# Two transformer blocks on one core: the second feed-forward in interleaved blocks of three, its later value chunks transposed by VectorE

## The chip, the core and the metric

One program runs on one core of a Trainium2 chip. The metric is the device time of one execution in microseconds (us), lower is better. TensorE multiplies, VectorE (DVE) and ScalarE (ACT) work element by element, GpSimd (POOL) has little to do here, and SyncE (SP) issues the transfers of the weights. Each engine takes its instructions in the order in which the program lists them, and waits on semaphores for the others.

## The reference, cut to what matters

Two blocks follow each other on 256 tokens of width 2048, in float32. The second block ends with a feed-forward part, and the change lies wholly in it:

```python
def conv_ffn(h, w_up, conv_w, conv_b, w_down):      # h: 256 x 2048
    u = h @ w_up                                    # w_up: 2048 x 11264
    ...
    y = conv_b                                      # causal, width 3, each channel by itself
    for i in range(CONV_WIDTH_2):
        y = y + conv_w[i] * u_pad[:, i:i + S]
    gate, val = jnp.split(y, 2, axis=-1)            # 5632 channels each
    return (jax.nn.silu(gate) * val) @ w_down       # w_down: 5632 x 2048
```

Its result is added to `x`, and that is the output.

## The kernel before

**Chunks, tiles, units, steps.** Every matrix product is cut into chunks of 512 output columns (`CW`), which accumulate in one of two PSUM buffers (`acc`). A chunk's contraction is cut into tiles of 512 rows of weights, and each tile into two units of 256 rows. A unit has two steps of 128 rows. An up chunk (512 columns of `w_up`) has 4 tiles, so 8 units and 16 steps; the 22 up chunks come in pairs, a gate chunk `g` and a value chunk `v` with the same index j from 0 to 10. A pair makes 512 of the 5632 rows that the down product contracts over (`d0` to `d10`). A down chunk is 512 columns of `w_down` over the rows of one block of pairs, with one tile for each pair of the block.

**Precision.** All products are made of float32r parts: the weights are split into `wh` (rounded, a copy by ScalarE, line 846) and `wl` (what is left, a subtraction by VectorE, line 847), the left-hand side in the same way into the two halves of a tile `k_...`. Of each step, TensorE issues six products of 512 columns (line 887): four with `wh`, then two with `wl`. The split of a unit is put into the program three units before its products (`SPLIT_AHEAD = 3`); `wh`, `wl` and the raw weights have four buffers each.

**The order of the other work.** `later(delay, fn)` puts a piece of work on a heap, due so many steps from now; after each step at most three due pieces are put into the program (`run_due`). At the end of a chunk its `evac` is put in, ahead of what is due. `need` puts in everything up to a key at once. The place of an instruction in the engine's queue is fixed by this, long before the kernel runs.

**What an up chunk leaves to do** (`evac_up`): ScalarE copies the accumulator to `z` with the tokens on the partitions (line 440). Then `z` is transposed, since the convolution and the down product want the channels there. This is done in one of two ways:

- `transposed`: TensorE makes four 128 x 128 transposes at a time into a PSUM tile `p_t` (line 175), two such groups for a chunk, due 3 and 5 steps after its end (2 and 3 for the last value chunk, `soon`).
- `turned`: VectorE makes 16 transposes of 32 x 256 into an SBUF tile `z_t` (line 190), two after each step from the second on (`rate=2`).

The convolution follows for each half of the chunk: ScalarE's part (line 479), four operations of VectorE (line 484). For a gate chunk comes a sigmoid by ScalarE (line 745) and a product by VectorE (line 746). For a value chunk comes the product with the gate (VectorE, line 740) and the split into the `k_d` tile (ScalarE line 155, VectorE line 162). Before the change all gate chunks are `turned` and all value chunks `transposed`.

**A down chunk** leaves one addition by VectorE of 128 x 1024 elements to the residual `x` (`evac_add`, line 543). The last chunk of the program is computed half by half (`acc_last`, lines 893 to 895 and 540).

**The order of chunks** is that of the calls of `add_chunk`: four pairs, then four down chunks of 4 tiles; four pairs, four down chunks of 4 tiles; three pairs, four down chunks of 3 tiles.

Of the kernel before, what the change touches and what calls it, by code (L numbers as in the profile page):

```python
# [26 lines left out]
FF2 = 5632  # L27
EPS = 1e-6
NEG = -1e30
CW = 512  # L30
# [31 lines left out]
def tile_two_blocks(  # L62
# [30 lines left out]
    def later(delay, fn, *keys):  # L93
        seq[0] += 1
        heapq.heappush(tasks, (now[0] + delay, seq[0], fn, keys))

    def chain(delay, stages, *keys, gap=1):

        for i, fn in enumerate(stages):
            later(delay + i * gap, fn, *(keys if i == len(stages) - 1 else ()))  # L100
# [11 lines left out]
    def need(*keys):  # L112
        for key in keys:
            while key not in ready:
                run_one()
# [21 lines left out]
    def add_chunk(w, row0s, c0, ncol, acts, evac):  # L137

        chunks.append((w, row0s, c0, ncol, acts, evac))
# [7 lines left out]
    def split_out(key, j, n, p, scales=None):  # L147

        if key not in K:
            kt_tile(key)  # L150
        hi, lo = (K[key][:, h, j:j + n, :] for h in range(2))

        def to_hi():
            if scales is None:
                S.copy(hi, p)
            else:
                for i in range(n):
                    S.activation(hi[:, i, :], p[:, i, :], AF.Copy, scale=scales[i])

        def to_lo():  # L160
            if scales is None:
                V.tensor_tensor(out=lo, in0=p, in1=hi.bitcast(F32), op=OP.subtract)  # L162
            else:
                for i in range(n):
                    V.scalar_tensor_tensor(out=lo[:, i, :], in0=p[:, i, :], scalar=scales[i],  # L165
                                           in1=hi[:, i, :].bitcast(F32), op0=OP.mult, op1=OP.subtract)
        return [to_hi, to_lo]

    def transposed(z, use, delay, keys=(), gap=1, lag=1, step=1):

        def task(b, mine):
            p = tr_p.tile([P, 2, T], F32, tag="tr", name="p_t")
            for j in range(2):
                for tb in range(TB):
                    TE.transpose(p[:, j, tb * P:(tb + 1) * P], z[:, tb, (2 * b + j) * P:(2 * b + j + 1) * P], ident)  # L175
            chain(lag, use(b, p), *mine, gap=step)
        for b in range(2):
            later(delay + gap * b, lambda b=b: task(b, keys[2 * b:2 * b + 2]))

    def turned(z, use, delay, keys, rate=3, lag=1):  # L180

        t = {}

        def part(i0, i1):
            if i0 == 0:
                t["o"] = z_p.tile([P, 4, T], F32, tag="z", name="z_t")
            for q, j in [divmod(i, 4) for i in range(i0, i1)]:
                src = z[32 * q:32 * q + 32].rearrange("p b (k c) -> p b k c", c=P)[:, :, :, 32 * j:32 * j + 32]
                dst = t["o"][32 * j:32 * j + 32].rearrange("p k (b t) -> p b k t", b=TB)[:, :, :, 32 * q:32 * q + 32]
                V.transpose(dst, src)  # L190

        def rest():
            for b in range(2):
                chain(lag + b, use(b, t["o"][:, 2 * b:2 * b + 2, :]), *keys[2 * b:2 * b + 2])
        n = 0
        for i in range(0, 16, rate):
            later(delay + n, lambda i=i: part(i, min(i + rate, 16)))
            n += 1
        later(delay + n - 1, rest, keys[0] + " turned")

    def group_keys(key):
        return [f"{key} {j}" for j in range(4)]
# [174 lines left out]
    hT = lambda name: [f"{name}{n}" for n in range(4)]  # L377
# [57 lines left out]
    def evac_scaled(rname, then, mult=None):  # L435

        def evac(acc):
            z = z_p.tile([P, TB, CW], F32, tag="z", name="z")
            for tb in range(TB):
                S.activation(z[:, tb, :], acc[:, tb, :], AF.Copy, scale=R[rname][:, tb:tb + 1])  # L440
            then(z)
        return evac
# [32 lines left out]
    def conv3(o, u, w, bias):  # L475

        def last():
            for i in range(2):
                S.activation(o[:, i, :], u[:, i, :], AF.Identity, bias=bias(i), scale=w(i, 2))

        def before():
            for i in range(2):
                for d in (1, 2):
                    V.scalar_tensor_tensor(out=o[:, i, d:T], in0=u[:, i, 0:T - d], scalar=w(i, 2 - d), in1=o[:, i, d:T],  # L484
                                           op0=OP.mult, op1=OP.add)
        return [last, before]
# [50 lines left out]
    def evac_add(n, then=None):  # L537
        def evac(acc, tb=None):
            if tb is not None:
                V.tensor_tensor(out=xs[n][:, tb, :], in0=xs[n][:, tb, :], in1=acc, op=OP.add)  # L540
                nc.sync.dma_start(outr[:, tb, n * CW:(n + 1) * CW], xs[n][:, tb, :])
                return
            V.tensor_tensor(out=xs[n], in0=xs[n], in1=acc, op=OP.add)
            if then:
                then(n)
        return evac
# [182 lines left out]
    def evac_up(which, j, key):  # L729
        def then(z):  # L730
            cv = z_p.tile([P, 4, T], F32, tag="z", name="z_cv")

            def use(b, p):
                a = cv[:, 2 * b:2 * b + 2, :]
                c0 = (0 if which == "g" else 44) + 4 * j + 2 * b
                steps = conv3(a, p, lambda i, t: ccol[:, t, c0 + i:c0 + i + 1], lambda i: ccol[:, 3, c0 + i:c0 + i + 1])
                if which == "v":
                    g = FU["g", j][:, 2 * b:2 * b + 2, :]
                    need(f"gate{j} {2 * b}")
                    return steps + [lambda: V.tensor_tensor(out=a, in0=a, in1=g, op=OP.mult), *split_out(key, 2 * b, 2, a)]  # L740
                t = {}

                def sigmoid():
                    t["s"] = s_p.tile([P, 2, T], F32, tag="s", name="sg")
                    S.activation(t["s"], a, AF.Sigmoid)
                return steps + [sigmoid, lambda: V.tensor_tensor(out=a, in0=a, in1=t["s"], op=OP.mult)]
            if which == "g":
                FU["g", j] = cv
            if which == "g":
                turned(z, use, 2, group_keys(f"gate{j}"), rate=2)  # L750
            else:
                soon = j == FF2 // CW - 1
                transposed(z, use, 2 if soon else 3, group_keys(key), gap=1 if soon else 2)
        return then


# [2 lines left out]
    G4 = [0, 512, 1024, 1536]  # L759
# [27 lines left out]
    for blk in range(4):  # L787
        for i in range(4):
            j = 4 * blk + i
# [18 lines left out]
    def store(n):  # L808
        nc.sync.dma_start(outr[:, :, n * CW:(n + 1) * CW], xs[n])

    j = 0
    for cnt in (4, 4, 3):
        js = list(range(j, j + cnt))
        j += cnt
        for jj in js:
            add_chunk(w_up_2[0], G4, jj * CW, CW, hT("g"), evac_scaled("r4", evac_up("g", jj, f"d{jj}")))
            add_chunk(w_up_2[0], G4, FF2 + jj * CW, CW, hT("g"), evac_scaled("r4", evac_up("v", jj, f"d{jj}")))
        for n in range(4):
            add_chunk(w_down_2[0], [jj * CW for jj in js], n * CW, CW, [f"d{jj}" for jj in js],
                      evac_add(n, store if j == 11 else None))  # L820


    wtiles = []
# [137 lines left out]
```

## Time and profile before

| | us |
|---|---|
| median of 3 runs (2393.58 to 2395.01) | 2394.24 |
| the profiled execution's own time | 2393.52 |
| its span, first to last instruction | 2391.8 |
| TensorE busy in the span | 2362.4 |
| VectorE busy | 1662.8 |
| ScalarE busy | 1159.0 |

The second feed-forward runs from 1654 us of the span to its end. Times in the profile are counted from the start of the span; the 1.7 us between the span and the execution's own time lie outside it. A matmul's end is modelled, so the distance of two starts is a better measure of TensorE than its busy time.

### The profile page before, as it was taken

The page shows a single profiled execution, that of the slowest core. Times are in us where ns is not written, and L with a number is a line of the kernel's source. Part 1 is how long each engine was busy: PE and PEld are TensorE (multiplying, and loading weights), DVE is VectorE, ACT ScalarE, POOL GpSimd, SP SyncE. Part 2 cuts the span into 40 slices and gives each one's busy share as a digit, 9 for nine tenths or more (in the row PEclk, how much of TensorE's full clock was granted, in tenths as well). Part 3 has the DMA queues.
Part 4 walks back from the last instruction along what each step waited for, and adds up shares of the span by engine and source line. Part 5 has one row for each costly group of instructions (what it writes and reads, how often), then busy time and mean ns, then how long its engine had stood idle before and what let it go on. Part 6 is the DMA issues. An engine that isn't in the chain of part 4 may idle for free.

```text
span 2391.8 us, 27807 instructions
## 1 busy us (share of the span) xinstructions
PE 2362.4 (99%) x10649; PEld 1960.1 (82%) x10649; DVE 1662.8 (70%) x2293; ACT 1159.0 (48%) x1514; POOL 36.7 (2%) x53
## 2 busy tenths in 40 slices
PE   9899999999999999999999999999999999999999
PEld 9688888888888888888888888888888888888887
DVE  5487776665877567567578857668788568864884
ACT  5355454444455344344354455545555345554553
POOL 1000000000000000000000001000000000000000
PEclk9999999999999999999999999999999999999999
DMA  7755656655556556656555666555555656565553
GB/s 259 188 184 165 204 194 207 202 201 177 192 195 195 193 181 206 193 184 201 193 183 190 189 205 203 165 176 194 183 177 199 199 180 206 178 198 189 194 185 132
DMA packets 230966, 456.67 MB, mean 191 GB/s; under 512 B 8085, under 2 KB 15997, under 8 KB 230832
## 3 DMA queue, kind: packets, MB, share of 16 engines
q1 hardware_dynamic: 227584, 445.81, 56.7%
q0 software_dynamic: 3248, 9.08, 1.6%
q8 instruction: 83, 1.36, 0.2%
q14 instruction: 51, 0.42, 0.0%
HBM read 451.18 MB, written 3.67 MB: 190 GB/s over the span
## 4 chain that ended last, share of the span: by engine, by line
PE 91%; DVE 4%; DMA 2%; ACT 1%; issue 1%; SPq 0%; POOL 0%; ACTq 0%; DVEq 0%
PE acc L887 89%; DMA raw<-in_w_in_dram 2%; DVE wl L847 2%; DVE z_t L190 1%; ACT wh L846 1%; PE p_t L175 1%; PE acc_last L887 0%; DVE z_cv L484 0%; PE p_t L360 0%; PE p_s L316 0%; PE p_t L714 0%; DVE k_i L165 0%; PE p_p L351 0%; ACT junk L227 0%; DMA bg<-in_g_final_dram 0%
## 5 line engine op out<-in xcount | busy, mean ns | idle before, releaser
L847 DVE TENSOR_TENSOR wl<-raw,wh 128x1024 fp32r<-128x1024 f32 (+1 forms) x848 | 1021.6, 1214 | 635.1 <-ACT wh L846 546.5
L846 ACT CAST wh<-raw 128x1024 fp32r<-128x1024 f32 (+1 forms) x848 | 876.5, 1044 | 713.6 <-PE acc L887 648.9
L887 PE MATMUL acc<-wh,k_g 128*128 128x512 f32 x1408 | 378.4, 390 | 0.0
L887 PE MATMUL acc<-wh,k_h 128*128 128x512 f32 (+1 forms) x1344 | 352.2, 384 | 12.6 <-ACT wh L846 12.2
L887 PEld LDWEIGHTS acc<-wh,k_g 128*128 128x128 f32 x1408 | 263.0, 188 | 53.8
L887 PEld LDWEIGHTS acc<-wh,k_h 128*128 128x128 f32 x1344 | 247.2, 189 | 58.3 <-ACT wh L846 13.5
L887 PE MATMUL acc<-wh,k_u 128*128 128x512 f32 x1024 | 274.8, 390 | 4.5 <-DVE k_u L162 4.5
L887 PE MATMUL acc<-wh,k_f 128*128 128x512 f32 x1024 | 273.9, 389 | 0.0
L887 PEld LDWEIGHTS acc<-wh,k_u 128*128 128x128 f32 x1024 | 191.9, 188 | 45.9 <-DVE k_u L162 6.2
L887 PEld LDWEIGHTS acc<-wh,k_f 128*128 128x128 f32 x1024 | 192.1, 188 | 39.8
L887 PE MATMUL acc<-wl,k_g 128*128 128x512 f32 x704 | 216.9, 389 | 0.0
L887 PE MATMUL acc<-wl,k_h 128*128 128x512 f32 (+1 forms) x672 | 201.1, 380 | 0.1
L887 PE MATMUL acc<-wh,k_d 128*128 128x512 f32 x656 | 176.3, 390 | 1.5 <-DVE k_d L162 1.5
L887 PE MATMUL acc<-wl,k_u 128*128 128x512 f32 x512 | 157.7, 389 | 0.0
L887 PE MATMUL acc<-wl,k_f 128*128 128x512 f32 x512 | 157.6, 389 | 0.0
L887 PEld LDWEIGHTS acc<-wl,k_g 128*128 128x128 f32 x704 | 132.1, 188 | 27.8
L190 DVE STREAM_TRANSPOSE z_t<-z 32x256 f32<-32x256 f32 x336 | 146.3, 435 | 5.6
L887 PEld LDWEIGHTS acc<-wh,k_d 128*128 128x128 f32 x656 | 122.6, 188 | 27.1 <-DVE k_d L162 1.9
L887 PEld LDWEIGHTS acc<-wl,k_h 128*128 128x128 f32 x672 | 125.0, 188 | 23.6 <-DVE wl L847 0.7
L887 PE MATMUL acc<-wh,k_i 128*128 128x512 f32 x512 | 141.0, 398 | 0.6 <-ACT wh L846 0.6
L190 DVE STREAM_TRANSPOSE z_t<-z_f 32x256 f32<-32x256 f32 x256 | 111.4, 435 | 4.1
L887 PEld LDWEIGHTS acc<-wl,k_u 128*128 128x128 f32 x512 | 96.1, 188 | 20.0
(227 smaller groups left out, 2006.3 us busy)
## 6 DMA issues: line engine op xcount, KB each, us to landing
raw<-in_w_ff_dram SPq DMA_DIRECT2D x128, 1024.0 KB, 5.2
raw<-in_w_in_dram SPq DMA_DIRECT2D x104, 1024.0 KB, 5.1
raw<-in_w_up_dram SPq DMA_DIRECT2D x88, 1024.0 KB, 5.1
raw<-in_w_down_dram SPq DMA_DIRECT2D x44, 1024.0 KB, 5.2
raw<-in_w_mix_out_dram SPq DMA_DIRECT2D x16, 1024.0 KB, 5.1
raw<-in_w_out_dram SPq DMA_DIRECT2D x16, 1024.0 KB, 5.1
raw<-in_w_conv_out_dram SPq DMA_DIRECT2D x8, 1024.0 KB, 5.2
raw<-in_w_attn_out_dram SPq DMA_DIRECT2D x8, 1024.0 KB, 5.3
```

What stands on the lines that cost most here:

```text
L175: TE.transpose(p[:, j, tb * P:(tb + 1) * P], z[:, tb, (2 * b + j) * P:(2 * b + j + 1) * P], ident)
L190: V.transpose(dst, src)
L846: S.copy(wh[:, :, 0:ncol], raw)
L847: V.tensor_tensor(out=wl[:, :, 0:ncol], in0=raw, in1=wh[:, :, 0:ncol].bitcast(F32), op=OP.subtract)
L887: TE.matmul(halves[tb][:, 0:ncol], k[:, i, kt, tb * P:(tb + 1) * P], w[:, kk, 0:ncol], start=begin and first and kt == 0, stop=end and stop)
```

## The change

Two things are changed. The order of chunks: the pairs form blocks of three (0 to 2, 3 to 5, 6 to 8, and 9 and 10); after the first block, each following pair of up chunks is followed by one down chunk of the block before, and what is left of the four down chunks comes behind the block's last pair. The down chunks of the first three blocks have 3 tiles (12 steps), those of the last block 2 tiles (8 steps). And the value chunks from j = 3 on are `turned` (VectorE) instead of `transposed` (TensorE); the three before keep TensorE, and the special case for the last one is gone.

```diff
             if which == "g":
                 turned(z, use, 2, group_keys(f"gate{j}"), rate=2)
+            elif j >= 3:
+                turned(z, use, 2, group_keys(key), rate=2)
             else:
-                soon = j == FF2 // CW - 1
-                transposed(z, use, 2 if soon else 3, group_keys(key), gap=1 if soon else 2)
+                transposed(z, use, 3, group_keys(key), gap=2)
...
-    j = 0
-    for cnt in (4, 4, 3):
-        js = list(range(j, j + cnt))
-        j += cnt
-        for jj in js:
-            add_chunk(w_up_2[0], G4, jj * CW, CW, hT("g"), evac_scaled("r4", evac_up("g", jj, f"d{jj}")))
-            add_chunk(w_up_2[0], G4, FF2 + jj * CW, CW, hT("g"), evac_scaled("r4", evac_up("v", jj, f"d{jj}")))
+    def up_chunks(j):
+        add_chunk(w_up_2[0], G4, j * CW, CW, hT("g"), evac_scaled("r4", evac_up("g", j, f"d{j}")))
+        add_chunk(w_up_2[0], G4, FF2 + j * CW, CW, hT("g"), evac_scaled("r4", evac_up("v", j, f"d{j}")))
+
+    def down_chunk(js, n, then=None):
+        add_chunk(w_down_2[0], [j * CW for j in js], n * CW, CW, [f"d{j}" for j in js], evac_add(n, then))
+
+    blocks = [range(0, 3), range(3, 6), range(6, 9), range(9, 11)]
+    for j in blocks[0]:
+        up_chunks(j)
+    for done, js in zip(blocks, blocks[1:]):
         for n in range(4):
-            add_chunk(w_down_2[0], [jj * CW for jj in js], n * CW, CW, [f"d{jj}" for jj in js],
-                      evac_add(n, store if j == 11 else None))
+            if n < len(js):
+                up_chunks(js[n])
+            down_chunk(done, n)
+    for n in range(4):
+        down_chunk(blocks[3], n, store)
```

All lines below the first edit move down, by 1 to 8: the split lines 846 and 847 of before are 854 and 855 after it, the products' line 887 is 895.

The order of VectorE's queue at the point where a value chunk (j = 4) has ended and its down chunk runs, after the change; the first rows still belong to the pair's gate chunk (`wl` is a unit's weight split, `z_cv` the convolution's tile, line 746 the gate's product, line 190 the value chunk's transposes):

```order
L746 TENSOR_TENSOR z_cv<-z_cv,sg 128x512 x2
L855 TENSOR_TENSOR wl<-raw,wh 128x1024 x2
L190 STREAM_TRANSPOSE z_t<-z 32x2x4x32 x2
L855 TENSOR_TENSOR wl<-raw,wh 128x1024
L190 STREAM_TRANSPOSE z_t<-z 32x2x4x32 x4
```

In the kernel before, the corresponding rows of VectorE's queue, behind a gate chunk's products, in the second block of pairs:

```order
L746 TENSOR_TENSOR z_cv<-z_cv,sg 128x512 x2
L847 TENSOR_TENSOR wl<-raw,wh 128x1024 x4
L484 SCALAR_TENSOR_TENSOR z_cv<-p_t,ccol,z_cv 128x255
L484 SCALAR_TENSOR_TENSOR z_cv<-p_t,ccol,z_cv 128x254
```

So the transposes now stand two splits behind the gate's products, where four splits and then the convolution stood. Further on in the same down chunk, VectorE's queue after the change, from the split ahead of the convolution to the split behind it (line 543 is the down chunk's addition, line 740 the product with the gate):

```order
L855 TENSOR_TENSOR wl<-raw,wh 128x1024
L484 SCALAR_TENSOR_TENSOR z_cv<-z_t,ccol,z_cv 128x255
L484 SCALAR_TENSOR_TENSOR z_cv<-z_t,ccol,z_cv 128x254
L484 SCALAR_TENSOR_TENSOR z_cv<-z_t,ccol,z_cv 128x255
L484 SCALAR_TENSOR_TENSOR z_cv<-z_t,ccol,z_cv 128x254
L543 TENSOR_TENSOR x_96<-x_96,acc 128x1024
L740 TENSOR_TENSOR z_cv<-z_cv 128x512
L484 SCALAR_TENSOR_TENSOR z_cv<-z_t,ccol,z_cv 128x255
L484 SCALAR_TENSOR_TENSOR z_cv<-z_t,ccol,z_cv 128x254
L484 SCALAR_TENSOR_TENSOR z_cv<-z_t,ccol,z_cv 128x255
L484 SCALAR_TENSOR_TENSOR z_cv<-z_t,ccol,z_cv 128x254
L855 TENSOR_TENSOR wl<-raw,wh 128x1024
```

For a gate chunk, before and after, the eight convolution rows between the two splits stand without lines 543 and 740; for the value chunks from j = 3 on these two now stand among them. TensorE's queue in the kernel before, from the end of the last value chunk to the first products with its result (`k_d_16504`, `k_d_16850`, `k_d_17184` are d8, d9 and d10):

```order
L887 MATMUL acc<-wl,k_g_12312 128x512 x2
L887 MATMUL acc<-wh,k_d_16504 128x512 x4
L887 MATMUL acc<-wl,k_d_16504 128x512 x2
...
L175 MATMUL p_t<-cc,z 128x128 x4
L887 MATMUL acc<-wh,k_d_16504 128x512 x4
L887 MATMUL acc<-wl,k_d_16504 128x512 x2
L175 MATMUL p_t<-cc,z 128x128 x4
...
L887 MATMUL acc<-wl,k_d_16850 128x512 x2
L887 MATMUL acc<-wh,k_d_17184 128x512 x4
```

After the change no row of line 175 follows there, and three down chunks of the block before (36 steps) stand between the last value chunk and the first product with d10, where 8 steps stood.

## Rows read from the trace of the kernel before

**Rows 1.** The page of the profile: span, and the first line of its first part.

```profile
span 2391.8 us, 27807 instructions
...
PE 2362.4 (99%) x10649; PEld 1960.1 (82%) x10649; DVE 1662.8 (70%) x2293; ACT 1159.0 (48%) x1514; POOL 36.7 (2%) x53
```

**Rows 2.** Windows of four down chunks, then four pairs: length, busy us of each engine, clock, DMA.

```profile
1832.00:1919.00 87.00, 87.00 (x389) 72.02 (x388) 52.61 (x55) 40.35 (x44) 0.00 (x0) 1.00 0.59 194
1919.00:2098.00 179.00, 179.00 (x803) 148.19 (x802) 138.62 (x200) 92.75 (x118) 0.00 (x0) 1.00 0.56 188
```

**Rows 3.** Timeline of PE around the end of value chunk 1: start, length, instruction, count.

```profile
1744.18 1.07 PE L887 MATMUL acc<-wh,k_g 128*128 128x512 f32 x4
...
1746.90 1.07 PE L887 MATMUL acc<-wh,k_g 128*128 128x512 f32 x4
1747.81 0.62 PE L887 MATMUL acc<-wl,k_g 128*128 128x512 f32 x2
1748.26 0.60 PE L175 MATMUL p_t<-cc,z 128*128 128x128 f32 x4
...
1754.66 1.07 PE L887 MATMUL acc<-wh,k_g 128*128 128x512 f32 x4
```

**Rows 4.** Timeline of PE behind the last value chunk; idle time ahead stands in brackets.

```profile
2320.00 1.07 PE L887 MATMUL acc<-wh,k_d 128*128 128x512 f32 x4
...
2326.19 1.07 PE L887 MATMUL acc<-wh,k_d 128*128 128x512 f32 x4
...
2330.27 1.07 PE L887 MATMUL acc<-wh,k_d 128*128 128x512 f32 x4
...
2333.76 0.73 PE L887 MATMUL acc<-wh,k_d 128*128 128x512 f32 x2 [1.52 <-DVE k_d L162]
...
2334.80 1.08 PE L887 MATMUL acc<-wh,k_d 128*128 128x512 f32 x4
```

**Rows 5.** Timeline of DVE in value chunk 1, over the work that gate chunk 1 left.

```profile
1725.99 0.87 DVE L190 STREAM_TRANSPOSE z_t<-z 32x256 f32<-32x256 f32 x2
...
1737.37 0.89 DVE L190 STREAM_TRANSPOSE z_t<-z 32x256 f32<-32x256 f32 x2
1740.37 1.23 DVE L847 TENSOR_TENSOR wl<-raw,wh 128x1024 fp32r<-128x1024 f32 x1 [2.11 <-ACT wh L846]
1741.51 3.74 DVE L484 SCALAR_TENSOR_TENSOR z_cv<-z_t,ccol,z_cv 128x255 f32<-128x255 f32 x8
1745.17 1.22 DVE L847 TENSOR_TENSOR wl<-raw,wh 128x1024 fp32r<-128x1024 f32 x1
1746.31 1.29 DVE L746 TENSOR_TENSOR z_cv<-z_cv,sg 128x512 f32<-128x512 f32 x2
1747.51 1.22 DVE L847 TENSOR_TENSOR wl<-raw,wh 128x1024 fp32r<-128x1024 f32 x1
1749.06 2.36 DVE L847 TENSOR_TENSOR wl<-raw,wh 128x1024 fp32r<-128x1024 f32 x2 [0.33 <-ACT wh L846]
```

**Rows 6.** Timeline of DVE at a down chunk's addition near the end.

```profile
2371.73 1.22 DVE L543 TENSOR_TENSOR x<-x,acc 128x1024 f32<-128x1024 f32 x1 [0.86 <-PE acc L887]
2372.87 1.22 DVE L847 TENSOR_TENSOR wl<-raw,wh 128x1024 fp32r<-128x1024 f32 x1
```

**Rows 7.** Windows behind two waits of PE: clock 0.50 and 1.00 in the column PEclk.

```profile
1496.10:1499.50 3.40, 3.40 (x9) 2.63 (x8) 1.73 (x5) 2.66 (x7) 0.00 (x0) 0.50 0.80 286
2332.00:2336.00 4.00, 2.48 (x12) 1.85 (x11) 3.45 (x4) 1.65 (x3) 0.00 (x0) 1.00 0.33 126
```

**Rows 8.** Timeline of PE at a wait in the second block's attention stage.

```profile
1495.13 0.70 PE L360 MATMUL p_t<-pt,k_v 128*128 128x256 f32 x2 [1.90 <-ACT pt L355]
...
1495.81 1.79 PE L887 MATMUL acc<-wh,k_i 128*128 128x512 f32 x4
...
1500.23 1.07 PE L887 MATMUL acc<-wh,k_i 128*128 128x512 f32 x4
```

## The prediction, made before the change was run

> **What bounds the kernel now.** First the page: TensorE is busy for 2362.4 of 2391.8 us [rows 1], so a change gains only what it takes out of TensorE's queue or out of its waits. Then the windows, by stage: while down chunks run, VectorE is busy for 52.6 of 87 us, while pairs of up chunks run for 138.6 of 179 [rows 2]. VectorE has room on average; whether it has any at a given moment is another question, which only the timelines answer.
>
> TensorE's timeline gives the measure of a step: two steps from 1744.18 to 1746.90, so 1.36 us each [rows 3]. Around the two groups of transposes of value chunk 1, five steps last from 1746.90 to 1754.66, 7.76 us instead of 6.80: a value chunk's transposes cost TensorE 0.96 us. The last value chunk costs more: three steps from 2320.00 to 2326.19 take 6.19 us instead of 4.08 (2.11 more, since TensorE also waits for `z`), and two steps from 2330.27 to 2334.80 take 4.53 instead of 2.72 (1.81 more: the first product with d10 waits for its split on VectorE) [rows 4].
>
> VectorE's timeline shows how near the limit the work is that a `turned` chunk leaves. The split that ends at 1746.40 (1745.17 and 1.23) is wanted by the unit that starts at 1746.90, by the products of 1747.81 [rows 3, 5]: 1.41 us to spare, the least of the usual pair. From 1725.99 on, VectorE idles only for the 2.11 us in which it waits for ScalarE, which itself waits for the last transposes [rows 5].
>
> **What is taken away.** Eight value chunks (j = 3 to 10) leave TensorE's queue: seven of 0.96 us, and the last with its 2.11. The wait of 1.81 for d10 goes too, since 36 steps (49 us) of down products now lie between the last value chunk and d10's first use, where 8 steps lay. Together 6.72 + 2.11 + 1.81 = **10.6 us less**. The number of products, of weight bytes and of transfers is the same; the first three value chunks keep their cost. Four more additions to the residual (16 down chunks instead of 12) are VectorE's, at 1.14 us each, counted below where they stand.
>
> **What is added, and what it meets.** VectorE gets 16 transposes a value chunk, 8 x 16 in all, at 0.45 us each (two from 1725.99 take 0.87) [rows 5]: 7.2 us a chunk, 57 us in all. A pair with its down chunk is 44 steps, 59.8 us, so on average they fit. They don't stand where the room is: the value chunk's transposes come directly behind the gate chunk's leftover, and the down chunk in which they run is 12 steps long.
>
> I follow VectorE's queue through such a down chunk with the durations of rows 5, as if it began at 1744.18, where value chunk 1 ended. Up to here nothing differs.
> - The gate's leftover and the splits run as in the rows until 1749.06. There, one split later (1.14 us from start to start, as 1740.37 to 1741.51), at 1750.20, the first transposes can start. Those of the gate chunk started at 1725.99, which is 16 steps earlier by the chunk, at 1747.75 by this clock: 2.45 us late.
> - From the first to the last transpose the rows show no idle time: 1725.99 to 1738.26, so 12.27 us. The last ends at 1762.47.
> - ScalarE's part of the convolution and its `wh` follow, 2.11 us, as in the rows: 1764.58. Then come a split (1.14), four convolution operations (1.83, half of 1741.51 to 1745.17), the addition (1.14 us from start to start) [rows 6], the product with the gate (0.60, as each of the two at 1746.31) and four convolution operations (1.83). The next split starts at 1771.12 and ends at 1772.35.
> - That split serves the tenth unit counted from the down chunk's start: nine units of 2.72 us after 1744.18 is 1768.66, and its first product with `wl` comes 0.91 later, at 1769.57 [rows 3].
>
> So TensorE waits **2.78 us**, in the fourth unit of the chunk behind the down chunk. The same split of a gate chunk had 1.41 to spare; the difference of 4.19 is the late start (2.45) and the two operations that stand ahead of it now, addition and product (1.74). After the wait on d10 (idle 1.52) 1.81 us were lost [rows 4]: starting again costs up to 0.29, and I take 0.2. So 3.0 us a chunk, for eight chunks **24 us more**. Behind it stand a product, ScalarE's cast of `k_d` and the next `wh`; how far that makes the next unit late no row shows. It lies between nothing and one more VectorE product (0.60) a chunk; I take nothing, and keep 4.8 us for the upper end. Then only splits stand in the queue, and VectorE recovers before the next value chunk begins.
>
> **The clock.** A wait of 1.90 us in the attention stage, with short matmuls next to it, was followed by a stretch at a granted clock of 0.50, the 1.2 GHz level [rows 7, 8]: two steps from 1495.81 to 1500.23 took 4.42 us, so 1.70 us were lost. Behind the wait of 1.52 us for d10 the clock stayed at 1.00, the 2.4 GHz level [rows 4, 7]. The eight new waits are longer than either. The lost clock costs between nothing and 8 x 1.70 = 13.6 us; I take half, **6.8 us**, because each of the two rows decides it the other way and a step at half the clock gives VectorE time to catch up. The Trainium skill, "TensorE: Matmul & The Clock Gate", Part 1, says that the slow clock is the default and that only activity lifts it; by that rule the waits would cost the upper end rather than the middle.
>
> **The sum.** 2393.5 (this execution) - 10.6 + 24 + 6.8 = 2413.7; the median of the runs lies 0.7 above this execution, so **2414 us**, slower by 0.8%.
>
> **The rivals.**
> - *The lead of three units covers it* (faster). If VectorE's chain is at least 2.78 us shorter than I have it, nothing waits and 10.6 us are gained: 2383.6. For it speaks the average load [rows 2], and that before the change the same kind of work passed without a wait [rows 3, 5]; against it that the rows add up without idle time. The Trainium skill, "VectorE: DVE Perf Modes", section "The three transpose paths", puts VectorE's transpose of 128 x 128 in bf16 at 311 ns, ahead of TensorE's 390. By that figure a value chunk's eight squares would be an estimated 2.5 us of VectorE, and this rival would hold. The rows show 0.45 us for 32 x 256 in float32, sixteen times, so I give the rival little. A milder form: if only the late start (2.45) is not carried, 0.33 + 0.2 us a chunk remain, 4.2 in all, and the time is 2387.8. Chance of both: 0.10.
> - *Gain and loss cancel* (the same). It needs a loss of 1.3 us a chunk. If ScalarE's waits hide the addition and the product (1.74 less), 1.04 + 0.2 us remain, 9.9 in all: 2393.5. The order speaks against it, since both stand between the two splits, and the wait for ScalarE lies ahead of them. Chance 0.06.
> - *Slower without the clock*: 2394.2 - 10.6 + 24 = 2407.6. *Slower with it each time*: 2421.2, or 2426 with the late next unit.
>
> **Chances and range.** The forecast with part of the clock lost, or with none or all of it, holds 0.84. The shortest wait that I hold likely is 0.6 us below mine (one VectorE product hidden), without clock loss: 2402.8. So the range is 2402 to 2426. By less than 0.2% (4.8 us) the measurement does not tell a change from none. Faster 0.10, the same 0.06, slower 0.84.
>
> **What would show it.** In the profile after: no transposes of `z` on TensorE for the later value chunks, and no wait for d10; eight waits of TensorE for the weight split `wl`, each near 2.8 us, some 24.5 us after the end of a value chunk; VectorE without idle time from there back to the gate's convolution, but for ScalarE's 2 us; stretches at the lower clock behind some of the eight. The prediction is wrong if TensorE shows no waits for `wl` there (then it is faster), if they are half as long, or if it waits for something that I have not listed, as weights that arrive late or a buffer of `z`.

## The result, and the profile after

The changed kernel takes **2417.7 us** (median of 4 runs, 2415.5 to 2420.0) against 2393.9 for the kernel before; the ratio is 1.0101, with a 95% interval of 1.0088 to 1.0113. It is slower by 1.0%, 24 us.

The page of the changed kernel, in the lines of [rows 1]: the span grew by 24.0 us, TensorE's busy time by only 4.2. The rest, 19.8 us, is idle time of TensorE.

```profile
span 2415.8 us, 27822 instructions
...
PE 2366.6 (98%) x10585; PEld 1959.6 (81%) x10585; DVE 1721.3 (71%) x2425; ACT 1156.1 (48%) x1514; POOL 36.6 (2%) x53
```

Who waited for whom, from 1654 us to the end of the changed kernel (engine and line, what it waited for, total us, times, longest; PEld is TensorE's load of the left-hand side). There is no wait for `k_d` any more. TensorE now waits eight times for a weight split of VectorE:

```profile
PEld acc L895 <- DVE wl L855: 25.5, 10, 3.1
...
PE acc L895 <- DVE wl L855: 21.1, 8, 2.7
```

The groups of instructions of that stretch: TensorE still makes 24 transposes of `z` (the first three value chunks), where it made 88, and VectorE makes 304 of 32 x 256 (128 more):

```profile
L190 DVE STREAM_TRANSPOSE z_t<-z 32x256 f32<-32x256 f32 x304 | 132.4, 435 | 5.2
...
L175 PE MATMUL p_t<-cc,z 128*128 128x128 f32 x24 | 3.9, 276 | 0.3 <-ACT z L440 0.2
```

The fourth of the eight waits, on TensorE's timeline (compare [rows 3]). A step is still 1.36 us. From 2067.55 to 2076.73 (the first and the last row; the view ends at 2077, inside the last one) four steps took 9.18 us instead of 5.44, so 3.74 were lost around one wait:

```profile
2067.55 1.07 PE L895 MATMUL acc<-wh,k_g 128*128 128x512 f32 x4
2071.26 0.73 PE L895 MATMUL acc<-wl,k_g 128*128 128x512 f32 x2 [2.65 <-DVE wl L855]
2071.84 1.08 PE L895 MATMUL acc<-wh,k_g 128*128 128x512 f32 x4
...
2073.52 1.19 PE L895 MATMUL acc<-wh,k_g 128*128 128x512 f32 x4 [0.15 <-ACT wh L854]
2074.78 0.73 PE L895 MATMUL acc<-wl,k_g 128*128 128x512 f32 x2
...
2076.73 0.62 PE L895 MATMUL acc<-wh,k_g 128*128 128x512 f32 x2
```

VectorE over the same down chunk (compare [rows 5]). By the whole view, of which some rows are left out here, it goes from the gate's products to the late split with no idle time but 0.32 and 2.11 us for ScalarE, and the split of 2069.99 ends 0.05 us before TensorE starts at 2071.26:

```profile
2045.19 1.29 DVE L746 TENSOR_TENSOR z_cv<-z_cv,sg 128x512 f32<-128x512 f32 x2
...
2047.93 1.23 DVE L855 TENSOR_TENSOR wl<-raw,wh 128x1024 fp32r<-128x1024 f32 x1 [0.32 <-ACT wh L854]
2049.07 0.87 DVE L190 STREAM_TRANSPOSE z_t<-z 32x256 f32<-32x256 f32 x2
...
2063.46 1.23 DVE L855 TENSOR_TENSOR wl<-raw,wh 128x1024 fp32r<-128x1024 f32 x1 [2.11 <-ACT wh L854]
2064.60 1.91 DVE L484 SCALAR_TENSOR_TENSOR z_cv<-z_t,ccol,z_cv 128x255 f32<-128x255 f32 x4
2066.43 1.22 DVE L543 TENSOR_TENSOR x<-x,acc 128x1024 f32<-128x1024 f32 x1
2067.56 0.69 DVE L740 TENSOR_TENSOR z_cv<-z_cv 128x512 f32<-128x512 f32 x1
2068.16 1.91 DVE L484 SCALAR_TENSOR_TENSOR z_cv<-z_t,ccol,z_cv 128x255 f32<-128x255 f32 x4
2069.99 1.22 DVE L855 TENSOR_TENSOR wl<-raw,wh 128x1024 fp32r<-128x1024 f32 x1
2071.12 0.69 DVE L740 TENSOR_TENSOR z_cv<-z_cv 128x512 f32<-128x512 f32 x1
...
2073.50 1.23 DVE L855 TENSOR_TENSOR wl<-raw,wh 128x1024 fp32r<-128x1024 f32 x1 [1.09 <-ACT wh L854]
```

ScalarE behind the late split. Its cast of `k_d` starts at 2071.90, when the product of 2071.12 has ended, and its casts of `wh` come after that; the first of the four ends at about 2073.5, just ahead of TensorE's 2073.52 and of VectorE's split of 2073.50, which ends just ahead of TensorE's 2074.78:

```profile
2071.90 0.62 ACT L155 CAST k_d<-z_cv 128x512 fp32r<-128x512 f32 x1 [2.95 <-DVE z_cv L740]
2072.43 3.89 ACT L854 CAST wh<-raw 128x1024 fp32r<-128x1024 f32 x4
```

The fifth wait, where the clock fell. From 2131.13 to 2138.22 two steps took 7.09 us instead of 2.72, so 4.37 were lost:

```profile
2131.13 1.07 PE L895 MATMUL acc<-wh,k_g 128*128 128x512 f32 x4
2134.84 1.22 PE L895 MATMUL acc<-wl,k_g 128*128 128x512 f32 x2 [2.64 <-DVE wl L855]
2135.86 1.91 PE L895 MATMUL acc<-wh,k_g 128*128 128x512 f32 x4
...
2138.22 1.09 PE L895 MATMUL acc<-wh,k_g 128*128 128x512 f32 x4
```

The windows behind these two waits, in the columns of [rows 7]: the granted clock is 1.00 behind the fourth and 0.50 behind the fifth. Of the eight such windows six have 0.50. Read in the same way, the eight waits lost 4.2, 4.5, 4.6, 3.7, 4.4, 4.5, 3.7 and 4.3 us, 33.9 in all; the two of 3.7 are those at the full clock.

```profile
2071.40:2074.80 3.40, 3.18 (x13) 1.98 (x13) 2.31 (x4) 2.90 (x4) 0.00 (x0) 1.00 0.68 211
2134.60:2137.90 3.30, 3.06 (x7) 2.48 (x8) 2.21 (x4) 2.43 (x4) 0.00 (x0) 0.50 0.57 158
```

### The profile page after: what moved, and what is told of

Read it like the earlier page. It is cut to its first block, busy times and chain, and to the rows that moved or that the text cites. A ratio compares the mean times of both kernels' runs of the same rounds, so it can differ in the third digit from the quotient of the medians.

```text
span 2415.8 us, 27822 instructions
## 1 busy us (share of the span) xinstructions
PE 2366.6 (98%) x10585; PEld 1959.6 (81%) x10585; DVE 1721.3 (71%) x2425; ACT 1156.1 (48%) x1514; POOL 36.6 (2%) x53
## 3 DMA queue, kind: packets, MB, share of 16 engines
q8 instruction: 83, 1.36, 0.2%
## 4 chain that ended last, share of the span: by engine, by line
PE 84%; DVE 9%; issue 3%; ACT 3%; DMA 2%; SPq 0%; ACTq 0%; DVEq 0%
PE acc L895 81%; DVE z_t L190 3%; DVE wl L855 3%; DVE z_cv L484 2%; DMA raw<-in_w_in_dram 2%; ACT wh L854 2%; PE p_t L175 0%; ACT z_cv L479 0%; DVE x L543 0%; ACT z L440 0%; PE p_t L360 0%; DVE z_cv L740 0%; PE p_s L316 0%; PE p_t L714 0%; PE acc_last L895 0%
## 5 line engine op out<-in xcount | busy, mean ns | idle before, releaser
L895 PEld LDWEIGHTS acc<-wh,k_f 128*128 128x128 f32 x1024 | 192.1, 188 | 39.6
L190 DVE STREAM_TRANSPOSE z_t<-z 32x256 f32<-32x256 f32 x464 | 202.0, 435 | 7.8
L895 PE MATMUL acc<-wh,k_d 128*128 128x512 f32 x672 | 182.8, 394 | 0.0
L895 PEld LDWEIGHTS acc<-wh,k_d 128*128 128x128 f32 x672 | 128.4, 191 | 27.1
L895 PE MATMUL acc<-wl,k_d 128*128 128x512 f32 x336 | 105.5, 396 | 7.9 <-DVE wl L855 7.9
```

Source lines behind the costliest of these rows:

```text
L895: TE.matmul(halves[tb][:, 0:ncol], k[:, i, kt, tb * P:(tb + 1) * P], w[:, kk, 0:ncol], start=begin and first and kt == 0, stop=end and stop)
```

## The experiments

My theory is that of the prediction: the value chunk's transposes stand behind the gate chunk's leftover in VectorE's queue, in the short down chunk, and the lateness (2.45 us) and the two operations put between two splits (1.74 us) use up the lead of the splits. The rivals: the order of chunks costs by itself; VectorE's 57 us more cost wherever they stand; the addition, which waits for TensorE itself, blocks VectorE.

| run | median us | ratio to before (95%) |
|---|---|---|
| order of chunks alone | 2390.1 | 0.9986 (0.9977 to 0.9995) |
| transposes alone | 2472.9 | 1.0333 (1.0317 to 1.0349) |
| one transpose a step | 2382.5 | 0.9957 (0.9945 to 0.9970) |
| addition six steps later | 2404.9 | 1.0048 (1.0034 to 1.0062) |
| transposes start four steps later | 2389.7 | 0.9985 (0.9976 to 0.9994) |
| one transpose a step, all value chunks | 2401.2 | 1.0033 (1.0021 to 1.0046) |

The kernel before took 2393.2 us beside the first four and 2393.5 beside the last two.

**The order of chunks alone.** The changed kernel, with

```diff
-            elif j >= 3:
-                turned(z, use, 2, group_keys(key), rate=2)
```

> The interleaved order of chunks alone: all value chunks are transposed by TensorE, at 0.96 us each. My theory (VectorE's queue behind the value chunk's own transposes makes the waits): no wait of TensorE for wl; of the cost of the last value chunk 2.11 falls to 0.96 and the wait of 1.81 for d10 goes, 2.96 us less than the kernel before, 2391.0. The rival that the interleaved order itself costs (other order of weights, four more additions): above 2394, and 2417 if it is the whole cause.

Measured 2390.1, 3.1 less than before. The interleaving costs nothing and gives back about what the last value chunk lost (2.96 by the prediction). This is the only line of TensorE's own waits (without the loads) from 1654 us on in this kernel:

```profile
PE p_t L175 <- ACT z L440: 0.2, 1, 0.2
```

**The transposes alone.** The kernel before, with

```diff
+            elif j >= 3:
+                turned(z, use, 2, group_keys(key), rate=2)
             else:
                 soon = j == FF2 // CW - 1
```

> The transposes by VectorE alone, in the order of chunks of before. My theory: the value chunk's work now meets the next gate chunk's 16 steps without the light down chunk to recover in, and the first products with d3, d7 and d10 come 8 to 12 steps after their value chunk's end, which the turned chunk can't keep: waits of some 10 to 15 us at each of the three and 2 to 5 us at the other pairs, so about 2463, between 2440 and 2485. The rival that the transposes cost the same wherever they stand (3.0 us a chunk and the clock): 2417.

Measured 2472.9, over three times the loss of the whole change. TensorE's own waits in this kernel: the first products with a fresh `k_d` wait longest, and the splits are late as well.

```profile
PE acc L889 <- ACT k_d L155: 31.7, 4, 12.4
PE acc L889 <- DVE wl L849: 10.8, 5, 2.5
PE acc L889 <- DVE k_d L162: 9.6, 6, 2.2
PE acc L889 <- ACT wh L848: 8.3, 8, 1.4
```

So the same 128 transposes cost very differently by where they stand, and the order of chunks is what keeps their cost down. A fixed cost for each transposed chunk is ruled out.

**One transpose a step.** The changed kernel, with

```diff
             elif j >= 3:
-                turned(z, use, 2, group_keys(key), rate=2)
+                turned(z, use, 2, group_keys(key), rate=1)
```

> The changed kernel with the value chunks' transposes put in one after each step instead of two, so over 16 steps: they end in the next gate chunk, which has only weight splits for VectorE. The same work in all. My theory: no wait for wl, no lower clock, and the whole 10.6 us gained: 2383.3, faster than both. The rival that VectorE's 57 us more are too much in themselves, wherever they stand: near 2417, at best half of the 24 us back, 2405.

Measured 2382.5, 10.7 less than the kernel before: faster than both. VectorE's work is the same to the instruction, so its amount isn't the cause. On its timeline (the same value chunk as above) the addition is no longer between the splits; they stand 5.53 us apart (2055.24 to 2060.77) instead of 6.53. That alone is 1 us. With fewer transposes between them the splits also keep further ahead of TensorE: the split of 2060.77 serves the fourteenth unit from the value chunk's end, not the tenth, and ends at 2061.99, 2.94 us before the products that need it (last row):

```profile
2055.24 1.23 DVE L855 TENSOR_TENSOR wl<-raw,wh 128x1024 fp32r<-128x1024 f32 x1 [2.11 <-ACT wh L854]
2056.38 1.91 DVE L484 SCALAR_TENSOR_TENSOR z_cv<-z_t,ccol,z_cv 128x255 f32<-128x255 f32 x4
2058.33 0.69 DVE L740 TENSOR_TENSOR z_cv<-z_cv 128x512 f32<-128x512 f32 x1
2058.94 1.91 DVE L484 SCALAR_TENSOR_TENSOR z_cv<-z_t,ccol,z_cv 128x255 f32<-128x255 f32 x4
2060.77 1.22 DVE L855 TENSOR_TENSOR wl<-raw,wh 128x1024 fp32r<-128x1024 f32 x1
...
2064.93 0.62 PE L895 MATMUL acc<-wl,k_g 128*128 128x512 f32 x2
```

**The addition six steps later.** The changed kernel, with

```diff
-        add_chunk(..., evac_add(n, then))
+        add_chunk(..., evac_add(n, then) if then else add_later(n))
+
+    def add_later(n):
+        return lambda acc: later(6, lambda: evac_add(n)(acc))
```

> The changed kernel with the addition of a down chunk put in six steps after its end (for the first three blocks), so it no longer stands between the two splits. My theory: each of the eight waits is 1.14 us shorter, 1.66 instead of 2.80; 9.1 us less than the changed kernel, 2408.6 with the clock as it was, and down to 2398.4 if none of the shorter waits is followed by the lower clock (1.52 was not, 1.90 was). The rival that the addition, which itself waits for TensorE's last product of the down chunk, blocks VectorE and makes the whole wait: no waits, 2383 to 2385.

Measured 2404.9, 12.8 less than the changed kernel. The addition's place is a part of the wait, not the whole of it. Behind none of the eight waits did the clock fall, and for that case I had expected 2398.4, 6.5 less: the expectation took off six falls at the prediction's 1.70 us each, and a fall costs less than that. One of the eight waits:

```profile
2061.87 1.07 PE L898 MATMUL acc<-wh,k_g 128*128 128x512 f32 x4
2064.62 0.73 PE L898 MATMUL acc<-wl,k_g 128*128 128x512 f32 x2 [1.68 <-DVE wl L858]
2065.19 1.09 PE L898 MATMUL acc<-wh,k_g 128*128 128x512 f32 x4
...
2066.88 1.20 PE L898 MATMUL acc<-wh,k_g 128*128 128x512 f32 x4 [0.15 <-ACT wh L857]
...
2068.71 1.07 PE L898 MATMUL acc<-wh,k_g 128*128 128x512 f32 x4
```

The idle time fell from 2.65 to 1.68, by 0.97 where 1.14 was expected; three steps took 6.84 instead of 4.08, so 2.76 were lost where the changed kernel lost 3.74 at the full clock. Eight times 0.98 is 7.8 us. Of the other 5.0 the clock explains most (some 4 us, see below): each of the eight waits lost the same 2.7 to 2.8 us here, and over the stretch with all of them the clock was 1.00, where it was 0.98 in the changed kernel. Eight times 2.76 on top of the 2382.5 of the run before is 2404.6. This window of the kernel with the late addition, then that of the changed kernel:

```profile
1840.00:2360.00 520.00, 504.96 (x2198) 410.43 (x2197) 416.73 (x601) 250.00 (x301) 0.00 (x0) 1.00 0.57 187
```

```profile
1840.00:2360.00 520.00, 498.43 (x2145) 407.97 (x2144) 411.86 (x597) 244.80 (x298) 0.00 (x0) 0.98 0.55 183
```

**The transposes start four steps later.** The changed kernel, still two a step:

```diff
             elif j >= 3:
-                turned(z, use, 2, group_keys(key), rate=2)
+                turned(z, use, 6, group_keys(key), rate=2)
```

> The changed kernel, still two transposes after each step, but the first of them put in six steps after the value chunk's end instead of two. My theory: the transposes then stand behind the splits that the gate's leftover had delayed, VectorE is no longer 2.45 us late with them, and the convolution falls into the next gate chunk, past the addition: waits of at most 0.4 us a chunk instead of 2.8, no lower clock, 2383 to 2388. The rival that two transposes a step are too dense wherever they start: waits of 1.5 us or more, above 2398.

Measured 2389.7, a little above the 2383 to 2388 that I expected, and far below the rival's 2398. TensorE has no wait for `wl` of its own any more. But this run does not show the late start by itself: the addition, too, moved out from between the two splits, to 2051.47 among the transposes. In the run before, in which the addition alone was moved, 1.7 us of idle time stayed; by subtraction the later start takes those away. What remains, around a value chunk: three steps from 2065.28 to 2070.16 took 4.88 us instead of 4.08, so 0.80 lost; eight of them are 6.4, and 2382.5 with them is 2388.9. The first of the three steps lasts 1.67 us, as the step from 2071.84 to 2073.52 (1.68) did in the changed kernel: it is the late next unit, here without a wait ahead of it.

```profile
2065.28 1.08 PE L895 MATMUL acc<-wh,k_g 128*128 128x512 f32 x4
...
2066.95 1.21 PE L895 MATMUL acc<-wh,k_g 128*128 128x512 f32 x4
...
2070.16 1.07 PE L895 MATMUL acc<-wh,k_g 128*128 128x512 f32 x4
```

**One transpose a step for all value chunks.** The changed kernel, without the cases:

```diff
-            elif j >= 3:
-                turned(z, use, 2, group_keys(key), rate=2)
             else:
-                transposed(z, use, 3, group_keys(key), gap=2)
+                turned(z, use, 2, group_keys(key), rate=1)
```

> One transpose a step for all value chunks, the first three too, which have no down chunk behind them. My theory: in a pair without a down chunk (32 steps, 43.5 us) VectorE's queue is full to the brim (16 splits at 1.14, 32 transposes at 0.45, 16 convolution operations at 0.46, six products of 0.60: 43.6 us), so waits come back around each of the first three value chunks, some 5 to 6 us a chunk, against 2.9 us saved on TensorE: about 2396, between 2388 and 2406, slower than one transpose a step from j = 3 on. The rival that one transpose a step is gentle enough anywhere: 2379.5.

Measured 2401.2, 18.7 more than with TensorE for the first three. With the 2.9 us that TensorE's transposes of them cost, 21.6 us are lost around three chunks, 7.2 each. I had expected 5 to 6, from a queue of VectorE that is full. In 46 us of one such pair VectorE was busy for 39.6, so it was not full, and of TensorE's own waits most are for ScalarE's cast `wh`. The rows show one of them: ScalarE's part of the convolution waits 5.05 us for VectorE's transposes, the cast stands behind it, and TensorE waits for the cast. So even one transpose a step is too much where no down chunk follows, but by way of ScalarE's queue as well as VectorE's; how much each makes is not shown.

```profile
PE acc L893 <- ACT wh L852: 10.6, 9, 1.6
PE acc L893 <- DVE wl L853: 3.2, 6, 0.8
```

```profile
1744.31 1.09 ACT L479 ACTIVATE z_cv<-z_t,ccol 128x256 f32<-128x256 f32 x2 [5.05 <-DVE z_t L190]
1745.31 1.03 ACT L852 CAST wh<-raw 128x1024 fp32r<-128x1024 f32 x1
...
1746.39 1.20 PE L893 MATMUL acc<-wh,k_g 128*128 128x512 f32 x4 [0.87 <-ACT wh L852]
```

```profile
1744.00:1790.00 46.00, 41.86 (x178) 32.73 (x177) 39.58 (x63) 24.62 (x32) 0.00 (x0) 1.00 0.56 181
```

## Why the prediction was right, point by point

**What is taken away (10.6 us): right.** The order alone gave 3.1 of it (2.96 by the sum), and with the transposes spread, where no wait is left, the whole came out: 10.7. (Between the last value chunk and the first product with d10 lie 40 steps, not 36, since the tile of d9 comes first; there is no wait either way.)

**VectorE's queue (a wait of 2.78 us): right, row by row.** In the changed kernel the gate's products start at 2045.19 where they started at 1746.31 [rows 5], 298.88 later. With that shift the sum has the first transposes at 2049.08, the split ahead of the convolution at 2063.46 and the late split at 2070.00; the rows show 2049.07, 2063.46 and 2069.99. TensorE started 2.80 us later than its steps would have it (2067.55 and 0.91 is 2068.46, and it was 2071.26). The other seven waits are alike, with 2.63 to 2.65 us idle each. Of the named parts the addition was shown by itself (about 1 us). The late start was shown only together with it, as what is left when the addition's part is taken off; the product (0.60) was never moved alone. The row of 1745.17 has 1.22 where the prediction reads 1.23, which changes its sum by 0.01.

**Starting again and the next unit (0.2 us a chunk): too small.** This term of the sum was mis-sized. Around the wait at the full clock 3.74 us were lost, so 0.94 besides the 2.80. The next unit was late too: ScalarE's cast of `k_d` waits for VectorE's product behind the late split, the next `wh` stands behind the cast, and both TensorE's next `wh` and its next `wl` products start late (2073.52 and 2074.78). I had seen this chain, and set it to nothing with at most 0.60 for the upper end; it costs more than that. The run with the later start has it without a wait ahead of it, at 0.80, which leaves 0.14 for starting again. Over eight chunks the term came out 5.9 us too small.

**The clock (6.8 us, four falls of 1.70): the fall right, both sizes off.** Six of eight waits were followed by the 1.2 GHz level, not four, but a fall cost 4.37 - 3.74 = 0.63 us in the chunk shown, not 1.70. Behind the fall the two late products are hardly waited for, since TensorE is slower than VectorE then: of the 1.57 us lost after the wait, 0.94 were lost at the full clock as well. By this chunk the six falls cost some 4 us; the eight waits read one by one give the same, 33.9 us against 29.9 for eight at the full clock. That a slower TensorE lets VectorE catch up was in the prediction, as a reason for half; that it swallows the next unit's waits was not. The Trainium skill, "TensorE: Matmul & The Clock Gate", Part 1, has the slow clock as the default and activity as what lifts it; the prediction took from this that every wait would be followed by a fall, which agrees with six of the eight waits and not with the two behind which the clock stayed at 1.00.

**The sum.** 8 x 3.74 + 6 x 0.63 - 10.6 = 23.1, and 2393.5 with it is 2416.6; the profiled execution took 2417.7, and 2414 was forecast. The two wrong sizes, 5.9 too little and 3.0 too much, partly cancel, so that 2414 came within 4 us of the measurement is in part luck.

**The rivals.** That the lead of three units covers it was wrong by the eight waits. The figure of the Trainium skill that would have made it hold ("VectorE: DVE Perf Modes", "The three transpose paths", 311 ns for 128 x 128 in bf16) doesn't describe these transposes: 435 ns for each of the 32 x 256 in float32, two of which hold as much as one such square. The rival "gain and loss cancel" was close for the kernel with the addition moved, which is still slower by 0.5%, so the addition alone did not decide it.

## What to carry to other kernels

Work that is moved off the bottleneck engine is free only if its new engine has room where the work is put, not on average: follow that engine's queue in program order over one period, with durations from the trace, and compare each feed of the bottleneck with the time at which it is needed. Here, with a down chunk behind them, the same 16 transposes cost a chunk 3.7 us or more at two a step from the second step on, 0.8 at two a step from the sixth, and nothing at one a step, and the fastest kernel measured (2382.5 us) is the change with that one number altered; without a down chunk one a step cost 7.2. When a wait is found, count the unit behind it too, since what the late engine owes next is late as well.

## What the runs showed of the hardware

The in-order queue of VectorE was so regular that a sum of start-to-start distances from one profile gave the start of an instruction 25 us on within 0.01 us, in another program (2070.00 by the sum, 2069.99 in the trace).

The clock's reaction was not that regular. Waits of TensorE of 2.65 us idle were followed by the 1.2 GHz level six times in eight in one execution, and eight waits of 1.65 to 1.68 us (the addition six steps later) not once. What made the difference among the eight equal waits no run here shows.
